# In-projection of a hybrid layer: 15 of its 20 units issued from a timetable, weight differences kept between the halves

## The chip, the core and the metric

The kernel runs on one core of a Trainium2 chip. The core has a matrix engine (TensorE, PE in the rows), three engines for elementwise work (VectorE or DVE, ScalarE or ACT, GpSimd or POOL) and a queue that issues DMA transfers (SyncE, SP). Each engine takes its instructions strictly in the order in which they were put into its queue, so an instruction that waits holds up everything behind it. The metric is the device time of one execution in microseconds, the median over runs.

## The reference, cut to what matters

The reference is one layer over 2048 time steps of 1024 channels: a normalised input, one wide projection, three recurrent mixers, an output projection and a gated convolutional feed-forward part. The change stands in the wide projection and in the causal convolutions that follow it.

```python
h = rms_norm(x, norm_mix_pre[l])                                     # x: (1, 2048, 1024) float32
xm, om, im, fm, xr, yr, zs, xbcs, dts = split_cols(h @ w_in[l])
# mLSTM:  x_c = silu(causal_dwconv(x_m, conv_w, conv_b))             # four taps each
# RG-LRU: xc  = causal_dwconv(x_r, conv_w, conv_b);  ... gelu(y_r)
# SSD:    xbc = silu(causal_dwconv(xbc, conv_w, conv_b))
def rms_norm(x, g):
    return x * lax.rsqrt(jnp.mean(x * x, axis=-1, keepdims=True) + EPS) * g
```

## The kernel before, in words

The products are float32. Each operand is cut into a high part and a low part (`hi` on ScalarE, L132, and `lo`, the rest, L134), and three matmuls with a moving block of 128x512 make one product (`split3`, L109 to L111).

Columns that are needed with time along the free axis are computed in two halves of 1024 time steps (half one, half two), each in ten **units**, b = 0 to 9. A unit gives two blocks of 128 output channels for 1024 steps. It is a Strassen product in Winograd's form: seven products of size 128 x 512 over four depth steps, so 7 x 4 x 3 = 84 matmuls. The seven run in the order b11, b21, T4, T1, T2, b22, T3, named by their weights; X, Y, V and Z are the PSUM banks that they add into. T1 to T4 are differences of weight blocks (`sub`, L139, on VectorE): T1 = b12 - b11, T2 = b22 - T1, T4 = T2 - b21, T3 = b22 - b12. They depend on the weights alone, and both halves compute them.

Four times in a unit ScalarE copies a bank out of PSUM (`keep`, L369): p1 after product one, p5 after product four, u2 after five and u3 after seven. Product six adds into bank Z only after p5 has been copied, product seven into bank X only after u2. Four adds on VectorE (L420 to L440) make the unit's two blocks ca and cb.

Around this run, in the same queues:
- the causal convolution of the unit before: per block a scale with bias on ScalarE (L448), three taps on VectorE (L451; in half two also three short ones on the carried tail, L455), for most blocks a Silu on ScalarE (L766, L771), and a store to `PT` (L778);
- the weights of a later unit: two loads of 512 KB (`ra`, `rb`, L270, L272), four differences, seven `hi`, seven `lo`, the latter on GpSimd;
- in half one, units 1 to 8, one tile of the input for half two (`norm_tile`, L613): a load, a square with its sum and a square root on ScalarE (L94, L95), a scaling on VectorE (L622), eight 128x128 transposes on TensorE (L628), two products with the gain on VectorE (L629) and a store of 512 KB;
- in half two, units 0 to 8, one step each of the gates' computation (`gates`, L644).

The order in each queue is the work of a list scheduler in the kernel's framework. It knows estimated durations and the priority of an instruction, which is its place in the program; PSUM evictions are given a higher one (`high_priority`). `t_units` (L736) calls the units in turn, and `between(b)` (L911 for half one, L951 for half two) puts the tile or the gate step behind unit b.

Of the kernel before, what the change touches and what calls it, by code (L numbers as in the profile page):

```python
# [9 lines left out]
F32 = mybir.dt.float32  # L10
F32R = mybir.dt.float32r
AF = mybir.ActivationFunctionType
# [51 lines left out]
def tile_hymba_layer(ctx: ExitStack, tc: tile.TileContext, io, out, scr):  # L64
    nc = tc.nc
    PSUM = bass.MemoryType.PSUM

    const = ctx.enter_context(tc.tile_pool(name="const", bufs=1))

    def c_tile(shape, name, dt=F32):  # L70
        return const.tile(shape, dt, name=name, tag=name)
# [16 lines left out]
    def col(t, name, j=0, n=1):  # L88
        o = COLS[name][0] + j
        return t[:, o : o + n]  # L90
# [493 lines left out]
    def phase_i():  # L584
# [141 lines left out]
        def gate_consts(gp):  # L726
# [6 lines left out]
            nc.vector.tensor_scalar_mul(nsp8, sp8, -8.0)  # L733
            nc.vector.tensor_scalar_mul(sp8, sp8, 8.0)

        def t_units(half, tp, tu, between=None, tail=None, w=None):  # L736

            t0 = half * TH
            w = w or prod.weights(tp, io["win_u"][0], f"iw{half}_0", half == 1, ON_DVE if half else ())
            if half == 1:  # L740
                for k in range(4):
                    prod.block(1, k, "a22", nc.vector if k % 2 else nc.gpsimd)
            for b in range(10):
                nm = f"i{half}_{b}"
                if b > 0:
                    w = prod.weights(tp, io["win_u"][b], f"iw{half}_{b}")
                pair = prod.unit(tu, w, nm, None, half == 1 and b == 0)
                if between is not None:
                    between(b)
                if tail is not None and b == 9:  # L750
                    tail()
                for i, c_ in enumerate(pair):
                    blk = 2 * b + i
                    if blk < 4:
                        nc.sync.dma_start(scr["PT"][4 + blk, :, t0 : t0 + TH], c_)
                    if blk < 16:
                        wn, bn, cb = (
                            ("cmw", "cmb", blk) if blk < 4 else ("crw", "crb", blk - 4) if blk < 8
                            else ("csw", "csb", blk - 8)
                        )  # L760
                        u = conv(
                            tu, c_, [col(par, wn, 4 * cb + k) for k in range(4)], col(par, bn, cb),
                            tails[:, blk, :], half, f"{nm}u{i}",
                        )
                    if blk < 4:
                        nc.scalar.activation(u, u, AF.Silu)  # L766
                        dst = blk
                    elif blk < 8:
                        dst = 16 + blk - 4
                    elif blk < 16:  # L770
                        nc.scalar.activation(u, u, AF.Silu)  # L771
                        dst = blk
# [88 lines left out]
        def in_proj_0():  # L861
# [46 lines left out]
            cnt = ExitStack()  # L908
            nt = open_pool(cnt, "nt", "right")

            def between(b):  # L911
                if 0 < b < 9:
                    norm_tile(nt, NCH + b - 1, load_x(nt, NCH + b - 1, 1), 2)()
                elif b == 9:
                    cnt.close()
                    pools.append(open_pool(ctu, "npa0", "right"))
                    st.append(n_units(pools, 0, range(NA, 4), [pu], "pu", 6, NRAW0))
                    next(st[0])
# [20 lines left out]
        def in_proj_1():  # L939
            ctp, ctu = ExitStack(), wo_ctx  # L940
            tu = open_pool(ctu, "bpp", "right")
            prep_pool.append(tu)
            prod.cps, prod.ws = CPS, 14 if W_EARLY else 18
            cgp = ExitStack()
            tp = open_pool(ctp, "tp1")
            gp = open_pool(cgp, "gp0")
            steps = gates(0, gp, pu, "px")

            st, pools = [], []

            def between(b):  # L951
# [457 lines left out]
    NJ = NFF // 2  # L1409
    NU = 8  # L1410

    dram = ctx.enter_context(tc.tile_pool(name="dram", bufs=1, space=bass.MemoryType.DRAM))
    aS = dram.tile([NU, P, NJ, 7, P], F32, name="aS", tag="aS")
    W = {}
    A = {}
# [981 lines left out]
```

## Time and profile before

| | |
|---|---|
| median of three runs | 2641.61 us (2638.68 to 2641.89) |
| time of the profiled execution | 2638.97 us |
| its span, first to last instruction | 2637.1 us |
| busy: TensorE, VectorE, ScalarE, GpSimd | 93%, 75%, 53%, 29% of the span |
| mean granted clock of TensorE | 0.977 of full speed |

Busy shares are means over the whole program, in which the in-projection's two halves fill 0.5 ms. What bounds this part is read from its own stretches: for each stretch the busy time of each engine and the granted clock (PEclk, 1.00 is 2.4 GHz), and TensorE's waits with the instruction that ended each.

### The profile page before, as it was taken

Reading aid. Unit: us, or ns where it says so; the run is one execution under the profiler, and the core shown is the slowest. Engines: PE = TensorE matmul, PEld = TensorE weight load, DVE = VectorE, ACT = ScalarE, POOL = GpSimd, SP = SyncE. Lnnn points to the kernel's source line nnn. Section 1 sums busy time; section 2 is a strip of 40 time slices with the busy share of each in tenths; the row PEclk is TensorE's granted clock in tenths of the full one; section 3 lists DMA queues with packets and bytes.
Section 4 is the critical chain, followed back from the end, with each engine's and each line's share of the span. In section 5 each row is a group of like instructions: output and inputs, shape, how many; then the busy total and the mean of one; then the engine's idle time right before and its main releaser. Section 6 shows DMA issues by size and latency. Waiting matters only on the chain. (4 is left out here: it accounts for less than half of the span.)

```text
span 2637.1 us, 38638 instructions
## 1 busy us (share of the span) xinstructions
PE 2459.5 (93%) x13658; PEld 2122.8 (80%) x13658; DVE 1986.0 (75%) x3096; ACT 1404.5 (53%) x2480; POOL 759.5 (29%) x616
## 2 busy tenths in 40 slices
PE   8899979899889989999899999989999988999997
PEld 8677867778788878877688787768888878999997
DVE  6898688857889864465787988877877877556676
ACT  5546655445467676555544544554445455445443
POOL 5555444434344442122500000111010143003222
PEclk9999989999999999999999999999999999999999
DMA  7444643236566555475645655656666658768875
GB/s 249 142 164 138 201 148 130 93 122 196 167 177 188 170 187 172 156 245 178 218 152 163 198 191 192 222 193 215 196 187 208 190 192 316 228 209 269 278 264 200
DMA packets 316338, 507.79 MB, mean 193 GB/s; under 512 B 23616, under 2 KB 198976, under 8 KB 316144
## 3 DMA queue, kind: packets, MB, share of 16 engines
q1 hardware_dynamic: 315152, 502.17, 58.9%
q8 instruction: 107, 1.75, 0.3%
q0 software_dynamic: 704, 2.10, 0.2%
q10 hardware_dynamic: 288, 1.05, 0.1%
q14 instruction: 87, 0.71, 0.1%
HBM read 337.72 MB, written 167.51 MB: 192 GB/s over the span
## 5 line engine op out<-in xcount | busy, mean ns | idle before, releaser
L997 POOL TENSOR_TENSOR yn<-yn,yg 128x512 f32<-128x512 f32 x16 | 22.1, 1380 | 149.4 <-DMA yg<-gate 93.2
L2209 POOL TENSOR_TENSOR o<-o,y 128x512 f32<-128x512 f32 x14 | 24.3, 1737 | 124.7 <-DVE y L2208 25.2
L109 PE MATMUL mix<-wo,ym 128*128 128x512 f32 x128 | 51.9, 405 | 1.6 <-DVE ysl L1028 1.6
L111 PE MATMUL mix<-wo,ym 128*128 128x512 f32 x128 | 50.9, 398 | 0.0
L110 PE MATMUL mix<-wo,ym 128*128 128x512 f32 x128 | 50.6, 395 | 0.0
L110 PE MATMUL mix<-wol,ysh 128*128 128x512 f32 x128 | 50.2, 392 | 0.1
L111 PE MATMUL mix<-woh,ysl 128*128 128x512 f32 x128 | 49.9, 390 | 0.0
L109 PE MATMUL mix<-woh,ysh 128*128 128x512 f32 x128 | 49.5, 392 | 0.2 <-ACT woh L580 0.2
L2103 POOL TENSOR_TENSOR d_0l<-d_0r,d_0h 128x768 fp32r<-128x768 f32 x2 | 4.1, 2074 | 145.7 <-DVE e_6y L2185 144.2
L1510 DVE TENSOR_TENSOR bh<-hT,g 128x512 f32<-128x512 f32 x32 | 20.7, 684 | 31.8 <-PE hT L1509 31.8
L999 DVE TENSOR_TENSOR yn<-yn,yg 128x1024 f32<-128x1024 f32 x16 | 21.3, 1330 | 22.0 <-ACT yg L998 22.0
L1028 DVE TENSOR_TENSOR ym<-yT,ym 128x512 fp32r<-128x512 f32 x16 | 11.0, 689 | 34.3 <-ACT ym L1027 34.3
L2118 ACT ACTIVATE e_8h<-e_8a 128x896 fp32r<-128x896 f32 x15 | 14.3, 954 | 36.9 <-DMA e_8a<-aS 28.8
L2119 DVE TENSOR_TENSOR e_10l<-e_10a,e_10h 128x896 fp32r<-128x896 f32 x15 | 16.4, 1090 | 23.3 <-ACT e_10h L2118 23.2
L1499 ACT ACTIVATE bt<-bx 128x1024 f32<-128x1024 f32 x16 | 16.9, 1059 | 29.4 <-DVE bx L1498 29.4
L852 ACT ACTIVATE no<-n 128x256 f32<-128x256 f32 x64 | 23.8, 374 | 16.2 <-PE n L111 5.9
L628 PE MATMUL xT<-ident,x 128*128 128x128 f32 x128 | 20.3, 305 | 12.8 <-DVE x L622 8.4
L629 DVE TENSOR_TENSOR hT<-xT,par 128x512 f32<-128x512 f32 x32 | 21.4, 683 | 13.6 <-PE xT L628 13.6
L998 ACT ACT_TABLE_LOAD x16 | 20.5, 1283 | 19.7 <-DMA yg<-gate 19.5
L2119 DVE TENSOR_TENSOR e_6l<-e_6a,e_6h 128x896 fp32r<-128x896 f32 x15 | 23.9, 1590 | 8.6 <-ACT e_6h L2118 8.6
L2119 DVE TENSOR_TENSOR e_5l<-e_5a,e_5h 128x896 fp32r<-128x896 f32 x15 | 23.2, 1547 | 8.6 <-ACT e_5h L2118 8.6
L2119 DVE TENSOR_TENSOR e_9l<-e_9a,e_9h 128x896 fp32r<-128x896 f32 x15 | 16.4, 1090 | 17.6 <-ACT e_9h L2118 17.6
(11864 smaller groups left out, 10855.1 us busy)
## 6 DMA issues: line engine op xcount, KB each, us to landing
x<-in_x_dram SPq DMA_DIRECT2D x16, 512.0 KB, 5.9
hT<-hT SPq DMA_DIRECT2D x16, 512.0 KB, 4.2
gate<-no SPq DMA_DIRECT2D x64, 128.0 KB, 2.9
yn<-yns SPq DMA_DIRECT2D x16, 512.0 KB, 4.7
yg<-gate SPq DMA_DIRECT2D x16, 512.0 KB, 5.1
bx<-in_x_dram SPq DMA_DIRECT2D x16, 512.0 KB, 5.1
x<-bx SPq DMA_DIRECT2D x16, 512.0 KB, 2.9
h2T<-bh SPq DMA_DIRECT2D x16, 512.0 KB, 5.0
```

The lines of the kernel that those rows point to most:

```text
L109: a = nc.tensor.matmul(pss, lh, rh, start=first, stop=False, skip_group_check=True)
L110: nc.tensor.matmul(pss, lh, rl, start=False, stop=False, skip_group_check=True)
L111: nc.tensor.matmul(pss, ll, rh, start=False, stop=last, skip_group_check=True)
L628: nc.tensor.transpose(pt[:, j * P : (j + 1) * P], xt[:, k * P : (k + 1) * P], ident)
L629: nc.vector.tensor_tensor(hT[:, 4 * q : 4 * q + 4], pt.rearrange("p (a b) -> p a b", a=4), col(par, "g1", 4 * q, 4).unsqueeze(2).to_broadc ...
L852: nc.scalar.activation(o, pt[:, 0:256], AF.Copy)
L997: nc.gpsimd.tensor_tensor(yn[:, 512:], yn[:, 512:], g[:, 512:], op=ALU.mult)
L998: nc.scalar.activation(g, g, AF.Sigmoid)
L999: nc.vector.tensor_tensor(yn, yn, g, op=ALU.mult)
L1510: nc.vector.tensor_tensor(hT[:, q * 4 : q * 4 + 4, :], pt.rearrange("p (a b) -> p a b", a=4), g2[:, 4 * q : 4 * q + 4].unsqueeze(2).to_bro ...
L2119: nc.vector.tensor_tensor(al, a, ah.bitcast(F32), op=ALU.subtract)
L2209: nc.gpsimd.tensor_tensor(o[i][:, hs], o[i][:, hs], t, op=ALU.add)
```

## The change

Units 1 to 8 of half one and 1 to 7 of half two no longer go through the scheduler. `timed_units` gives each instruction a time in slots: a slot is one depth step of a product (three matmuls), 28 slots make a unit, `t0` is a unit's start and `t1` its end. All instructions are sorted by these times and issued in that order, as it stands, to their engines' queues (`manual_schedule`). With that:
- all of a unit's evictions, convolutions and stores, the weights of the next unit (prepared 28 slots ahead), the input tiles and the gate steps stand at fixed slots;
- `lo` is computed on VectorE, except that of b11 in half one, which stays on GpSimd;
- the tile's eight transposes stand inside product six, and its gains are eight 128x128 copies with a column scale on ScalarE instead of two products on VectorE;
- in half one the differences T1 to T4 of the units prepared by the timetable (2 to 9) are also stored to DRAM (`iT`, 256 KB each); in half two those of units 2 to 8 are loaded instead of computed, and the fourth weight block b12 is not loaded.

Unit 0 and unit 9 of both halves and unit 8 of half two stay with the scheduler. The matmuls themselves and their order are unchanged.

```diff
--- before.py
+++ after.py
+        iT = dram.tile([10, P, 4, 512], F32, name="iT", tag="iT")
+        def timed_units(half, tp, tu, units, between, w):
...
+            def unit_events(b):
+                t0 = 28 * b
+                t1 = t0 + 28
...
+                for q, (bk, wn, hn, first) in enumerate((
+                    ("X", "b11", "a11", True), ("Y", "b21", "a12", True), ("V", "T4", "a22", True),
+                    ("Z", "T1", "s1", True), ("X", "T2", "s2", False), ("Z", "b22", "s4", False),
+                    ("X", "T3", "s3", False),
+                )):
+                    for k in range(4):
+                        at(t0 + 4 * q + k, step, bk, wn, hn, first, k)
...
+                at(t0 + 4, keep, "p1", "X")
+                at(t0 + 9.8, c_of, 0)
+                at(t0 + 9.9, evac, 0, 0, "Y", "p1")
+                at(t0 + 16, keep, "p5", "Z")
+                at(t0 + 20, keep, "u2", "X")
+                at(t0 + 24.1, c_of, 1)
+                at(t0 + 24.2, evac, 1, 0, "Z", "u2")
+                at(t1, keep, "u3", "X")
+                at(t1, evac, 1, 1, "X", "p5")
+                at(t1 + 0.9, evac, 0, 1, "u3", "V", ALU.subtract)
...
+                for i, (tc0, taps, tf) in enumerate(((2, (4.2, 6.1, 8.0), 10.2), (3.8, (12.4, 14.3, 16.2), 18.3))):
+                    blk = 2 * b + i
+                    if blk < 4:
+                        at(t1 + 2 + i, store, i, 4 + blk, "c")
...
+                    at(t1 + tc0, conv0, i, blk)
+                    for sh in (1, 2, 3):
+                        at(t1 + taps[sh - 1], tap, i, blk, sh)
+                    if blk < 4 or blk >= 8:
+                        at(t1 + tf, func, i, AF.Silu)
+                    at(t1 + tf + 1.6, store, i, blk if blk < 4 or blk >= 8 else 16 + blk - 4, "u")
...
+            def weight_events(b):
+                t0 = 28 * (b - 1)
...
+                at(t0 - 14, load, "ra", slice(0, 2), ("b11", "b21"))
+                at(t0 - 12, load, "rb", slice(2, 3 if half else 4), ("b22",) if half else ("b22", "b12"))
+                if half:
+                    for i, t in ((4, -11), (1, -8), (2, 3), (3, 10)):
+                        at(t0 + t, load_t, i)
+                    names = ("T4", "T1", "b11", "b21", "T2", "b22", "T3")
+                    his, los = (-1, 2.5, 5.5, 9, 13, 17, 20.5), (1.8, 3.6, 10.8, 11.6, 18.1, 20, 25.2)
+                else:
+                    at(t0 + 1.8, diff, "T1", "b12", "b11")
+                    at(t0 + 2.6, diff, "T2", "b22", "T1")
+                    at(t0 + 3.4, diff, "T4", "T2", "b21")
+                    at(t0 + 20.2, diff, "T3", "b22", "b12")
+                    at(t0 + 5.1, store_t, 1, 2, 4)
+                    at(t0 + 21.2, store_t, 3)
+                    names = ("b11", "b21", "T4", "T1", "T2", "b22", "T3")
+                    his, los = (-2, 3, 5, 9, 12.5, 17, 21.5), (-1, 10.8, 11.6, 18.1, 21.2, 22, 25.2)
+                for i, (name, th, tl) in enumerate(zip(names, his, los)):
+                    at(t0 + th, hi, name)
+                    at(t0 + tl, lo, name, nc.vector if i or half else nc.gpsimd)
+            for b in units:
+                unit_events(b)
+                between(b, at)
+            for b in units[1:]:
+                weight_events(b)
+            weight_events(units[-1] + 1)
+            with tc.manual_schedule():
+                for _, _, f, args in sorted(ev, key=lambda e: e[:2]):
+                    f(*args)
+            return W_[units[-1] + 1]
...
+            timed = range(1, 8 if half else 9)
             for b in range(10):
                 nm = f"i{half}_{b}"
-                if b > 0:
+                if b == 1:
+                    w = prod.weights(tp, io["win_u"][1], f"iw{half}_1")
+                    w = timed_units(half, tp, tu, timed, between, w)
+                if b in timed:
+                    continue
...
-                    norm_tile(nt, NCH + b - 1, load_x(nt, NCH + b - 1, 1), 2)()
...
+                    def scale():
+                        nc.vector.reciprocal(xn["ss"], xn["ss"])
+                        nc.vector.tensor_scalar_mul(xn["x"], xn["x"], xn["ss"])
+                    def transposes(q):
+                        xn[q] = pu.tile([P, 512], F32, name=f"xT{tt}_{q}", tag="px", bufs=2)
+                        for j in range(4):
+                            k = q * 4 + j
+                            nc.tensor.transpose(
+                                xn[q][:, j * P : (j + 1) * P], xn["x"][:, k * P : (k + 1) * P], ident
+                            )
+                    def gains(q):
+                        if q == 0:
+                            xn["h"] = nt.tile([P, KT, P], F32, name=f"hT{tt}", tag="hT", bufs=2)
...
+                            nc.scalar.activation(
+                                xn["h"][:, k], xn[q][:, j * P : (j + 1) * P], AF.Copy, scale=col(par, "g1", k)
+                            )
...
+                    at(t0 - 2, load)
+                    at(t0 + 7, square)
+                    at(t0 + 19, scale)
+                    at(t0 + 22.5, transposes, 0)
+                    at(t0 + 23.5, transposes, 1)
+                    at(t0 + 24.3, gains, 0)
+                    at(t0 + 25.8, gains, 1)
+                    at(t0 + 29, store)
...
+                if at is not None:
+                    at(28 * b + 22, next, steps, None)
+                    return
```

ScalarE in half one, while TensorE is in products four to seven of unit 6; iw0_7 are the weights of unit 7, i0_5 and i0_6 units 5 and 6. Before:

```order
L132 ACTIVATE iw0_7T2h_2220<-iw0_7T2_2208 128x512
L771 ACT_TABLE_LOAD
L771 ACTIVATE i0_5u0_1998<-i0_5u0_1998 128x1024
L369 ACTIVATE i0_6p5_2111<-i0_6Z_2058 128x512
L771 ACTIVATE i0_5u1_2006<-i0_5u1_2006 128x1024
L132 ACTIVATE iw0_7b22h_2224<-iw0_7rb_2196 128x512
L132 ACTIVATE iw0_7T3h_2230<-iw0_7T3_2228 128x512
L369 ACTIVATE i0_6u2_2125<-i0_6X_2056 128x512
```

Now:

```order
L871 ACTIVATE iw0_7T1h_2166<-iw0_7T1_2110 128x512
L820 ACT_TABLE_LOAD
L820 ACTIVATE i0_5u0_2112<-i0_5u0_2112 128x1024
L871 ACTIVATE iw0_7T2h_2186<-iw0_7T2_2117 128x512
L773 ACTIVATE i0_6p5_2204<-i0_6Z_2181 128x512
L871 ACTIVATE iw0_7b22h_2212<-iw0_7rb_2016 128x512
L820 ACTIVATE i0_5u1_2127<-i0_5u1_2127 128x1024
L773 ACTIVATE i0_6u2_2229<-i0_6X_2101 128x512
L871 ACTIVATE iw0_7T3h_2238<-iw0_7T3_2231 128x512
L1119 ACTIVATE hT13_2263<-xT13_0_2245,par_114 128x128 x4
```

The first Silu of unit 5 and the high part of T2 changed places, the second Silu went behind the high part of b22, and the first four of the eight gains (hT13) follow T3.

VectorE in half two, from behind the first add of unit 5 to the second (i1_5cb, now i1_5c1). Before:

```order
L451 SCALAR_TENSOR_TENSOR i1_4u1_4389<-i1_4cb_4270,par_112,i1_4u1_4389 128x1023
L455 SCALAR_TENSOR_TENSOR i1_4u1_4389<-tails_115,par_112,i1_4u1_4389 128x1
L451 SCALAR_TENSOR_TENSOR i1_4u1_4389<-i1_4cb_4270,par_112,i1_4u1_4389 128x1022
L455 SCALAR_TENSOR_TENSOR i1_4u1_4389<-tails_115,par_112,i1_4u1_4389 128x2
L451 SCALAR_TENSOR_TENSOR i1_4u1_4389<-i1_4cb_4270,par_112,i1_4u1_4389 128x1021
L455 SCALAR_TENSOR_TENSOR i1_4u1_4389<-tails_115,par_112,i1_4u1_4389 128x3
L139 TENSOR_TENSOR iw1_7T1_4743<-iw1_7rb_4733,iw1_7ra_4731 128x512
L139 TENSOR_TENSOR iw1_7T2_4745<-iw1_7rb_4733,iw1_7T1_4743 128x512
L139 TENSOR_TENSOR iw1_7T4_4747<-iw1_7T2_4745,iw1_7ra_4731 128x512
L139 TENSOR_TENSOR iw1_7T3_4765<-iw1_7rb_4733 128x512
L434 TENSOR_TENSOR i1_5cb_4440<-i1_5Z_4443,i1_5u2_4510 128x512
```

Now:

```order
L874 TENSOR_TENSOR iw1_6b11l_4554<-iw1_6ra_4436,iw1_6b11h_4553 128x512
L874 TENSOR_TENSOR iw1_6b21l_4574<-iw1_6ra_4436,iw1_6b21h_4573 128x512
L807 SCALAR_TENSOR_TENSOR i1_4u1_4540<-i1_4c1_4499,par_114,i1_4u1_4540 128x1023
L811 SCALAR_TENSOR_TENSOR i1_4u1_4540<-tails_117,par_114,i1_4u1_4540 128x1
L807 SCALAR_TENSOR_TENSOR i1_4u1_4540<-i1_4c1_4499,par_114,i1_4u1_4540 128x1022
L811 SCALAR_TENSOR_TENSOR i1_4u1_4540<-tails_117,par_114,i1_4u1_4540 128x2
L807 SCALAR_TENSOR_TENSOR i1_4u1_4540<-i1_4c1_4499,par_114,i1_4u1_4540 128x1021
L811 SCALAR_TENSOR_TENSOR i1_4u1_4540<-tails_117,par_114,i1_4u1_4540 128x3
L874 TENSOR_TENSOR iw1_6T2l_4600<-iw1_6T2_4537,iw1_6T2h_4599 128x512
L874 TENSOR_TENSOR iw1_6b22l_4625<-iw1_6rb_4448,iw1_6b22h_4624 128x512
L709 TENSOR_TENSOR lf0_4320<-bc0_4321,mst0_4486 4x1024
L779 TENSOR_TENSOR i1_5c1_4666<-i1_5Z_4590,i1_5u2_4641 128x512
```

The four differences of unit 7 (L139) are gone. Four low parts of unit 6's weights (L874) stand around unit 4's taps, and the first row of a gate step (L709) ahead of the second add.

SP's queue in half one, the transfers issued for one unit. Before:

```order
L270 DMA iw0_6ra_2014<-in_win_u_dram 128x1024
L272 DMA iw0_6rb_2016<-in_win_u_dram 128x1024
L609 DMA x11_1796<-in_x_dram 128x1024
L640 DMA hT_58<-hT10_1626 128x8x128
L778 DMA PT_59<-i0_3u0_1640 128x1024
L778 DMA PT_59<-i0_3u1_1647 128x1024
```

Now:

```order
L852 DMA iw0_6ra_1816<-in_win_u_dram 128x1024
L852 DMA iw0_6rb_1827<-in_win_u_dram 128x1024
L823 DMA PT_59<-i0_3u1_1749 128x1024
L865 DMA iT_120<-iw0_5T3_1851 128x512
L610 DMA x12_1899<-in_x_dram 128x1024
L1124 DMA hT_58<-hT11_1883 128x8x128
L865 DMA iT_120<-iw0_6T1_1920 128x512
L865 DMA iT_120<-iw0_6T2_1927 128x512
L865 DMA iT_120<-iw0_6T4_1935 128x512
L823 DMA PT_59<-i0_4u0_1922 128x1024
```

Four stores of differences (iT) joined the six transfers. The load of the input tile (x12) stands behind the store of T3 and a store of the unit-3 block.

## Rows read from the trace of the kernel before

**Rows 1.** Stretches of the in-projection; columns named in the fence's first line
```profile
core 0: us, PE busy (x) PEld busy (x) DVE busy (x) ACT busy (x) POOL busy (x), PEclk, DMA share, GB/s
102.64:277.06 174.42, 164.17 (x737) 131.88 (x736) 144.30 (x153) 99.74 (x146) 91.93 (x55) 1.00 0.46 151
256.81:277.06 20.25, 20.25 (x95) 16.53 (x94) 13.38 (x17) 13.51 (x19) 9.29 (x6) 1.00 0.55 168
391.52:575.66 184.14, 167.94 (x677) 133.39 (x678) 155.18 (x180) 90.45 (x129) 82.73 (x56) 0.93 0.28 102
391.52:397.20 5.68, 5.68 (x14) 4.48 (x15) 5.64 (x12) 0.54 (x1) 0.00 (x0) 0.51 0.19 76
440.36:459.80 19.44, 19.44 (x87) 15.90 (x86) 17.42 (x18) 9.19 (x13) 9.55 (x6) 1.00 0.34 107
459.80:479.09 19.29, 19.29 (x86) 15.77 (x84) 17.93 (x22) 9.12 (x14) 11.26 (x7) 1.00 0.23 85
```

**Rows 2.** TensorE's waits, half one, units 1 to 8; total, times, longest
```profile
PE i_1Z L109 <- ACT i_1p L369: 2.4, 1, 2.4
PE i_2Z L109 <- ACT i_2p L369: 1.8, 1, 1.8
...
PE i_5Z L109 <- ACT i_5p L369: 0.6, 1, 0.6
```

**Rows 3.** TensorE's waits before and in units 1 to 8, half two
```profile
PE i_1X L109 <- DVE i_0u L385: 6.9, 1, 6.9
PE i_5Z L109 <- ACT i_5p L369: 5.5, 1, 5.5
PE i_2Z L109 <- ACT i_2p L369: 2.8, 1, 2.8
...
PE i_7Z L109 <- ACT i_7p L369: 1.0, 1, 1.0
```

**Rows 4.** Order of time on ScalarE, half one, unit 6; start, duration
```profile
224.20 1.28 ACT L771 ACT_TABLE_LOAD   x1
...
226.46 0.58 ACT L369 ACTIVATE i_6p<-i_6Z 128x512 f32<-128x512 f32 x1
228.89 1.07 ACT L771 ACTIVATE i_5u<-i_5u 128x1024 f32<-128x1024 f32 x1 [1.85 <-DVE i_5u L451]
...
230.90 0.57 ACT L369 ACTIVATE i_6u<-i_6X 128x512 f32<-128x512 f32 x1
```

**Rows 5.** Order of time on VectorE, the same unit
```profile
221.33 1.27 DVE L451 SCALAR_TENSOR_TENSOR i_5u<-i_5cb,par,i_5u 128x1023 f32<-128x1023 f32 x1
222.53 2.31 DVE L451 SCALAR_TENSOR_TENSOR i_5u<-i_5ca,par,i_5u 128x1021 f32<-128x1021 f32 x1
...
228.86 0.67 DVE L139 TENSOR_TENSOR iw_8T<-iw_8rb,iw_8T 128x512 f32<-128x512 f32 x1
229.45 0.74 DVE L622 TENSOR_SCALAR x<-x,xss 128x1024 f32<-128x1024 f32 x1
```

**Rows 6.** Order of time on GpSimd, the same unit
```profile
222.13 1.62 POOL L134 TENSOR_TENSOR iw_7T1l<-iw_7T,iw_7T1h 128x512 fp32r<-128x512 f32 x1 [2.46 <-ACT iw_7T1h L132]
```

**Rows 7.** Order of time on ScalarE, half two, unit 6
```profile
523.39 1.06 ACT L771 ACTIVATE i_5u<-i_5u 128x1024 f32<-128x1024 f32 x1 [4.24 <-DVE i_5u L455]
...
524.87 0.58 ACT L369 ACTIVATE i_6u<-i_6X 128x512 f32<-128x512 f32 x1
```

**Rows 8.** A source line on VectorE; duration min/median/max
```profile
L166 DVE TENSOR_TENSOR iA_0a11a11l<-iA_2a,iA_0a11a11h x1: 680/680/680, 345.8 to 345.8; 128x512 fp32r<-128x512 f32 x1
```

**Rows 9.** A source line on ScalarE; duration min/median/max
```profile
L1222 ACT ACTIVATE m_0hs<-m_0pn,m_0dn x16: 346/367/375, 609.8 to 924.5; 128x128 f32<-128x128 f32 x16
```

**Rows 10.** VectorE's groups, half one, units 1 to 8; busy, mean, idle before
```profile
L629 DVE TENSOR_TENSOR hT<-xT,par 128x512 f32<-128x512 f32 x15 | 10.3, 685 | 12.4 <-PE xT L628 12.4
```

**Rows 11.** ScalarE's groups, the same stretch
```profile
L94 ACT ACTIVATE xj<-x 128x1024 f32<-128x1024 f32 x7 | 7.4, 1054 | 9.1 <-DMA x<-in_x_dram 9.1
```

**Rows 12.** DMA issues of the whole span; KB each, median us to landing
```profile
x<-in_x_dram SPq DMA_DIRECT2D x16, 512.0 KB, 5.9
```

More of the change, by code (lines that the diff above doesn't have):

```diff
@@ L68, in tile_hymba_layer @@
     const = ctx.enter_context(tc.tile_pool(name="const", bufs=1))
+    dram = ctx.enter_context(tc.tile_pool(name="dram", bufs=1, space=bass.MemoryType.DRAM))
     def c_tile(shape, name, dt=F32):
@@ L742, in t_units @@
                     prod.block(1, k, "a22", nc.vector if k % 2 else nc.gpsimd)
+            timed = range(1, 8 if half else 9)
             for b in range(10):
                 nm = f"i{half}_{b}"
-                if b > 0:
+                if b == 1:
+                    w = prod.weights(tp, io["win_u"][1], f"iw{half}_1")
+                    w = timed_units(half, tp, tu, timed, between, w)
+                if b in timed:
+                    continue
+                if b > timed[-1] + 1:
                     w = prod.weights(tp, io["win_u"][b], f"iw{half}_{b}")
@@ L909, in in_proj_0, with between, load, square @@
             nt = open_pool(cnt, "nt", "right")
-            def between(b):
+            def between(b, at=None):
                 if 0 < b < 9:
-                    norm_tile(nt, NCH + b - 1, load_x(nt, NCH + b - 1, 1), 2)()
+                    tt, xn = NCH + b - 1, {}
+                    t0 = 28 * b
+                    def load():
+                        xn["x"] = load_x(nt, tt, 1)
+                    def square():
+                        xn["ss"] = ip.tile([P, 1], F32, name=f"xss{tt}", tag="xss", bufs=4)
+                        jk = nt.tile([P, D], F32, name=f"xj{tt}", tag="xj", bufs=1)
+                        nc.scalar.activation(jk, xn["x"], AF.Square, accum_out=xn["ss"])
+                        nc.scalar.activation(xn["ss"], xn["ss"], AF.Sqrt, scale=1.0 / D, bias=epst)
+                    def scale():
[7 more added lines that the diff above has]
+                                xn[q][:, j * P : (j + 1) * P], xn["x"][:, k * P : (k + 1) * P], ident
+                            )
+                    def gains(q):
+                        if q == 0:
+                            xn["h"] = nt.tile([P, KT, P], F32, name=f"hT{tt}", tag="hT", bufs=2)
+                        for j in range(4):
+                            k = q * 4 + j
+                            nc.scalar.activation(
+                                xn["h"][:, k], xn[q][:, j * P : (j + 1) * P], AF.Copy, scale=col(par, "g1", k)
+                            )
+                    def store():
+                        nc.sync.dma_start(scr["hT"][:, :, tt * P : (tt + 1) * P].rearrange("k p t -> p k t"), xn["h"])
+                    at(t0 - 2, load)
[6 more added lines that the diff above has]
+                    at(t0 + 29, store)
                 elif b == 9:
@@ L949, in in_proj_1, with between @@
             st, pools = [], []
-            def between(b):
+            def between(b, at=None):
+                if at is not None:
+                    at(28 * b + 22, next, steps, None)
+                    return
                 next(steps, None)
@@ L1410, in tile_hymba_layer @@
     NU = 8
-    dram = ctx.enter_context(tc.tile_pool(name="dram", bufs=1, space=bass.MemoryType.DRAM))
     aS = dram.tile([NU, P, NJ, 7, P], F32, name="aS", tag="aS")
```

76 lines of the change are left out of this document (added).

## The prediction

> **What bounds the kernel now.** I read the stretches first, then TensorE's waits in them, then the order of time around a wait. The stretch of units 1 to 8 of half one lasts 174.42 us, with VectorE busy for 144.30 and ScalarE for 99.74; unit 8 alone, in which TensorE waits for nothing, takes 20.25 us with its tile's transposes in it [rows 1]. Half two's units 1 to 8 last 184.14 us, while two of them, without transposes, run in 19.44 and 19.29 us [rows 1]. So TensorE's own work is the floor of both halves, and the distance to it is 174.42 - 8 x 20.25 = 12.4 us in half one and 184.14 - 8 x 19.37 = 29.2 us in half two.
>
> What fills that distance: in half one seven waits, from 2.4 down to 0.6 us, 10.2 us together [rows 2]; the other 2.2 us are small gaps. In half two the seven waits inside units 1 to 8, from 5.5 to 1.0 us, make 16.3 us, and a further 6.9 us wait stands before unit 1 [rows 3]. The granted clock over half two's stretch is 0.93, in half one 1.00 [rows 1]: 0.07 x 184.14 = 12.9 us, which with 16.3 gives the 29.2. In the 5.68 us after the 6.9 us wait the clock is 0.51, near the lower of the two levels [rows 1]. Waits of up to 2.4 us in half one left the clock at 1.00; the lost clock belongs to half two's longer waits.
>
> Nearly all these waits are for a copy out of PSUM on ScalarE, and ScalarE is not busy then: it is blocked. In unit 6 of half one the copy i_6u starts at 230.90, behind a Silu that waited 1.85 us for a tap on VectorE [rows 4]. In half two the Silu at 523.39 waited 4.24 us and the copy i_6u came behind it [rows 7]. The taps are late because of their neighbours: a tap that takes 1.27 us takes 2.31 where a `lo` runs on GpSimd at the same time [rows 5, 6]. VectorE, stretched and in an unlucky order, sets the Silus; the Silus set ScalarE; ScalarE sets the banks.
>
> **The change part by part.** *lo from GpSimd to VectorE.* One `lo` on VectorE takes 0.68 us [rows 8]. Half one pays 6 x 0.68 = 4.1 us a unit for it, half two 7 x 0.68 = 4.8. What it gives back is the stretching, some 1.04 us for each tap that met one (2.31 - 1.27).
>
> *VectorE's sum per unit afterwards.* Half one: six taps at 1.27 = 7.6, four adds and four differences of the same shape at 0.67 = 5.4, six `lo` = 4.1, the scaling 0.74 [rows 5, 8], together 17.9 of 20.25 us; before it was busy 144.30 / 8 = 18.0 [rows 1], with the gains in it, two of 0.685 us [rows 10], which go. Half two: taps 7.6, adds 2.7, `lo` 4.8 = 15.1 us, and the tails and a gate step beside them in the remaining 4.3; before 155.18 / 8 = 19.4, all of its unit. The differences that are no longer computed take 4 x 0.67 = 2.7 us a unit off. So VectorE fits under TensorE in both halves, with more room in half two.
>
> *Gains on ScalarE.* The nearest row for a 128x128 copy with a column scale out of PSUM is 0.37 us [rows 9]; eight are 2.9 us. Unit 8's 13.51 us [rows 1] become 16.4 of 20.25. From both sides: a quarter of the 0.685 us that VectorE takes for 128x512 [rows 10] would make 1.4 us in all, 0.685 us each 5.5 and thus 19.0, still under the unit. I take 2.9. ScalarE's table loads stay as many as they were, at 1.28 us [rows 4]. The Trainium skill, "ScalarE: Activation LUTs", section "Rules for kernel authors", budgets about 2.7 us for each switch to another table set. Here a load is followed by its Silu within 1.29 us of its start [rows 4], so the trace disagrees; by the page two switches a unit would add 2.8 us and bring ScalarE to 19.2, with hardly any slack, which is the first rival's case.
>
> *The order.* By the slots a copy is due four slots (4 x 19.37 / 28 = 2.8 us) before TensorE needs its bank: p5 at 16, needed at 20; u2 at 20, needed at 24. Adding up durations in the order of each queue, I find p5 done about two slots and u2 about one and a half before they are needed in half one, earlier in half two. The tightest place is the tile: the scaling ends some 0.5 us before the transposes at slot 22.5. If the scaling is late, TensorE waits by as much in each of eight units.
>
> *DRAM instead of differences.* Half one adds four stores of 256 KB a unit, half two takes four loads and drops a quarter of `rb`. Half one moved 151 GB/s at a DMA share of 0.46 [rows 1], 3.3 MB a unit; with 1.0 MB more the share becomes about 0.6. The trace has no transfer of 256 KB like these. The nearest is 512 KB in 5.9 us to landing [rows 12]; from below, half of that. The loads stand ten slots (6.9 us) ahead of their first reader, so even at 5.9 us they are hidden: cost nothing. Without that cover it would be some 3 us a unit.
>
> *What stays.* The 6.9 us wait before unit 1 of half two hangs on unit 0's chain on VectorE, which the scheduler still orders, and the slow clock behind it: 5.68 x 0.49 = 2.8 us. Units 0 and 9 I leave as they are; unit 8 of half two is cheaper as its weights and unit 7's work no longer stretch VectorE.
>
> **Sum.** Half one -12.4. Half two -29.2 + 2.8 = -26.4. Against that I set 0.2 us a unit, some 3.2 us in all, for small slips, half the 0.5 us of the tile's margin. Together -35.6. From the profiled execution's 2638.97 us this is 2603.4; the median of the runs lies 2.6 us above the profiled execution, so 2606. The case's own range is 2596 to 2614.
>
> **Rivals.** *One: the timetable frees only half two.* In half one ScalarE takes 2.9 us more, and every Silu and the square still stand ahead of copies. If one slips, the fixed order can't give way: half one stays at 174.4. For it: VectorE at 17.9 of 20.25 leaves little room. Against it: both are under the floor. Time: -26.4 + 1.6 = -24.8, so 2617. Half one alone gained, with half two unchanged, is -12.4 + 1.6, so 2631: the loads from DRAM would have to come late.
>
> *Two: slower, by the tile's load.* The tile has one buffer. Its load can go out only when the transposes of the tile before are done, about 2.5 us before the unit's end, and it stands on SP behind the store of T3. With 5.9 us [rows 12] it lands 3.4 us into the unit. The square waits for it on ScalarE, and behind it stand T1's high part, the table load, a Silu, T2's and then p5, some 6.8 us of work, with p5 needed 13.6 us into the unit. So it decides from about 3.4 us of further lateness on; beyond that TensorE waits for each us in each of eight units. For it: before, the square already waited 9.1 us in seven units for this tile [rows 11], and the queue gets four more transfers a unit. Against it: a share of 0.6 leaves the DMA engines room. To end above the old time it must cost over 36 / 8 = 4.5 us a unit, a landing after 13.8 us or so; at 16 us it is 8 x 6.7 = 54 us on the 2606, or 2660.
>
> *Three: no gain.* What the in-projection gives back is lost behind it, because the recurrences wait for something else: 2642. Against it: TensorE is busy for 93% of the span and the next part takes its input from these units.
>
> **Chances.** The forecast 0.62, half two alone 0.20, half one alone 0.05, the slow tile 0.08, nothing 0.05. Faster by more than 0.2%, which is 5.3 us and about what a measurement of this kernel can tell from no change: 0.62 + 0.20 + 0.05 = 0.87; within it 0.05; slower 0.08. The range runs from 2592, if the 6.9 us wait and its slow clock shrink too and nothing slips (2638.97 - 38.8 - 9.7 + 2.6 = 2593), to 2631 with half two unchanged; the slow tile and part of no gain are left out.
>
> **What would show it.** Right: half one's units 1 to 8 near 162 to 164 us and half two's near 158 to 160, taps at 1.27 us throughout, no wait of TensorE for p5 or u2, and a granted clock of 1.00 behind the first 6 us of half two. A wait of the transposes for the scaling in each unit would put the allowance too low. Waits for ScalarE's copies in half one with ScalarE busy would speak for the first rival, a square that waits long for its tile for the second. I am wrong if the in-projection gets as short as this and the total doesn't follow.

## The result: 2641.75 to 2607.27 us

Over four runs each the kernel before has a median of 2641.75 us (2638.68 to 2645.34) and the changed one 2607.27 us (2605.82 to 2608.33), a ratio of 0.9863 with a 95% interval of 0.9843 to 0.9883. Measured again later, it had 2606.29 against 2643.68 us, 0.9851 (0.9821 to 0.9881). The forecast was 2606 us, its range 2592 to 2631. One execution of all those below, 7472 us for the kernel before with an unused DRAM tile, was a slow one and stands in no figure.

The stretches of units 1 to 8 in the changed kernel's profile, as in [rows 1], and the first 6 us of half two's stretch:

```profile
core 0: us, PE busy (x) PEld busy (x) DVE busy (x) ACT busy (x) POOL busy (x), PEclk, DMA share, GB/s
98.33:260.15 161.82, 161.82 (x738) 132.40 (x736) 137.20 (x191) 119.95 (x214) 10.35 (x8) 1.00 0.62 211
374.38:531.88 157.50, 157.12 (x677) 127.59 (x678) 130.13 (x203) 90.04 (x127) 4.73 (x4) 0.99 0.46 149
374.38:380.40 6.02, 6.02 (x20) 4.87 (x21) 5.14 (x8) 2.04 (x2) 0.00 (x0) 0.75 0.33 129
```

Half one's eight units take 161.82 us instead of 174.42, which is 8 x 20.23 with no wait of TensorE at all. Half two's take 157.50 instead of 184.14. ScalarE is busy for 119.95 / 8 = 15.0 us a unit in half one, VectorE for 137.20 / 8 = 17.2; GpSimd fell from 91.93 us to 10.35. TensorE's waits before and in half two's units, as in [rows 3]:

```profile
PE i_1X L110 <- DVE i_0u L386: 4.1, 1, 4.1
PE ptr L683 <- DVE r L685: 0.4, 1, 0.4
```

The wait of unit 1 is still there, 4.1 us instead of 6.9, and the clock behind it is 0.75 for 6.0 us instead of 0.51 for 5.7. ScalarE in unit 6 of half one, as in [rows 4], start and duration first:

```profile
205.47 1.05 ACT L1099 ACTIVATE xj<-x 128x1024 f32<-128x1024 f32 x1
...
208.75 1.28 ACT L820 ACT_TABLE_LOAD   x1
210.04 1.06 ACT L820 ACTIVATE i_5u<-i_5u 128x1024 f32<-128x1024 f32 x1
...
211.53 0.58 ACT L773 ACTIVATE i_6p<-i_6Z 128x512 f32<-128x512 f32 x1
...
213.50 1.06 ACT L820 ACTIVATE i_5u<-i_5u 128x1024 f32<-128x1024 f32 x1 [0.87 <-DVE i_5u L807]
214.47 0.58 ACT L773 ACTIVATE i_6u<-i_6X 128x512 f32<-128x512 f32 x1
...
216.10 2.17 ACT L1119 ACTIVATE hT<-xT,par 128x128 f32<-128x128 f32 x8
```

The first Silu starts without a wait at 210.04, and the copy i_6p follows at 211.53. The second Silu still waits 0.87 us for a tap, and the copy i_6u comes at 214.47; TensorE waits for neither copy. The eight gains take 2.17 us. VectorE in the same unit, as in [rows 5]:

```profile
203.69 3.92 DVE L807 SCALAR_TENSOR_TENSOR i_5u<-i_5c,par,i_5u 128x1023 f32<-128x1023 f32 x3
...
208.95 0.68 DVE L874 TENSOR_TENSOR iw_7T4l<-iw_7T,iw_7T4h 128x512 fp32r<-128x512 f32 x1
209.55 3.92 DVE L807 SCALAR_TENSOR_TENSOR i_5u<-i_5c,par,i_5u 128x1023 f32<-128x1023 f32 x3
...
214.18 0.75 DVE L1104 TENSOR_SCALAR x<-x,xss 128x1024 f32<-128x1024 f32 x1
```

Three taps in a row take 3.92 us, 1.31 each, with no 2.31 among them, and a `lo` takes 0.68. Of the 84 taps of units 1 to 7 in both halves 83 take 1.27 to 1.29 us and one 2.39. The scaling ends at 214.93 us; the transposes that need it start at 215.35, so the margin is 0.42 us.

Where the time came from, stage by stage, from the two profiled executions (the end of a stage is the next one's first matmul):

| stage | before | changed | difference |
|---|---|---|---|
| half one, unit 0 | 32.30 | 28.10 | -4.2 |
| half one, units 1 to 8 | 174.42 | 161.82 | -12.6 |
| half two, unit 0 and the wait behind it | 33.44 | 32.95 | -0.5 |
| half two, units 1 to 8 | 184.14 | 157.50 | -26.6 |
| end of half two's unit 9 | 595.12 | 551.34 | -43.8 |
| from there to the end of the span | 2041.98 | 2052.76 | +10.8 |

The stages that are not listed changed by 0.3 us or less. By the end of the in-projection 43.8 us are gained, 33.0 by the end of the span. Of the part behind, this is before's stretch in one row of the windows:

```profile
595.12:2637.10 2041.98, 1928.57 (x11046) 1678.75 (x11044) 1523.70 (x2538) 1086.60 (x1975) 469.66 (x409) 0.98 0.63 204
```

So 10.8 us seem to be given back where no engine's order differs. The experiments below ask whether that is so.

### The profile page after: what moved, and what is told of

Its sections match the earlier page's. It is cut to its first block, busy times and chain, and to the rows that moved or that the text cites. A ratio compares the mean times of both kernels' runs of the same rounds, so it can differ in the third digit from the quotient of the medians.

```text
span 2604.1 us, 38618 instructions
## 1 busy us (share of the span) xinstructions
PE 2451.1 (94%) x13658; PEld 2121.9 (81%) x13658; DVE 1953.2 (75%) x3149; ACT 1425.2 (55%) x2546; POOL 604.4 (23%) x519
## 5 line engine op out<-in xcount | busy, mean ns | idle before, releaser
L2431 POOL TENSOR_TENSOR o<-o,y 128x512 f32<-128x512 f32 x14 | 24.6, 1759 | 126.5 <-DVE y L2430 26.6
L1029 ACT ACTIVATE no<-n 128x256 f32<-128x256 f32 x64 | 23.9, 375 | 16.4 <-PE n L112 7.2
L110 PEld LDWEIGHTS mix<-wo,ym 128*128 128x128 f32 x128 | 24.5, 192 | 6.9 <-issue 1.7
L110 PEld LDWEIGHTS mix<-woh,ysh 128*128 128x128 f32 x128 | 24.2, 190 | 6.8 <-ACT woh L581 1.5
L2341 DVE TENSOR_TENSOR e_9l<-e_9a,e_9h 128x896 fp32r<-128x896 f32 x15 | 16.4, 1091 | 17.7 <-ACT e_9h L2340 17.6
```

Source lines behind the costliest of these rows:

```text
L110: a = nc.tensor.matmul(pss, lh, rh, start=first, stop=False, skip_group_check=True)
L1029: nc.scalar.activation(o, pt[:, 0:256], AF.Copy)
L2341: nc.vector.tensor_tensor(al, a, ah.bitcast(F32), op=ALU.subtract)
L2431: nc.gpsimd.tensor_tensor(o[i][:, hs], o[i][:, hs], t, op=ALU.add)
```

## The experiments

Theory one, the prediction's: a `lo` on GpSimd stretches VectorE's taps beside it, and moving it is what frees TensorE. Theory two: the fixed order frees it, and the placement only gives slack. "Half one" and "half two" below are units 1 to 8 of each.

**The changed kernel again**, unchanged, with a new profile.

> The changed kernel once more. In its first profile units 1 to 8 of half one took 161.8 us, those of half two 157.5, and from the end of the in-projection's last unit to the end of the span 2052.8 us, against 2042.0 before, though every engine's order there is the same. If the 10.8 us belong to the change, this profile has 2050 to 2055 there again; if they belong to that one execution, it lies near 2042 to 2047 and the total near 2600.

Measured: half one 161.81 us, half two 158.78, behind the in-projection 2053.9 us; the median of its four runs was 2606.29. The stages repeat, half two within 1.3 us.

**The kernel before again**, one run.

> The kernel before once more, for a second profile. Units 1 to 8 at 174.4 and 184.1 us and 2042 us behind the in-projection if these stages repeat; a spread of several us behind it would make the 10.8 us a matter of the execution.

Measured: 174.64 and 180.63 us, 2038.8 behind, 2632.6 us in all. Half two differs by 3.5 us from the first profile of the same kernel. Behind the in-projection before has 2042.0 and 2038.8 now, the changed kernel 2052.8 and 2053.9.

**The timetable alone**, with all placements of before.

```diff
-at(t0 + tl, lo, name, nc.vector if i or half else nc.gpsimd)
+at(t0 + tl, lo, name, nc.gpsimd)
-# gains(q): four nc.scalar.activation(hT[k], xT[k], AF.Copy, scale=g1[k])
+# gains(q): one nc.vector.tensor_tensor(hT[4q:4q+4], xT, g1[4q:4q+4], op=mult)
-at(t0 + t, load_t, i)                     # half two; and store_t in half one
+at(t0 - 3, diff, "T1", "b12", "b11"); ...  # differences computed in both halves
...                                        # b12 loaded in half two too, its first hi half a slot later
```

> The timetable alone: lo back on GpSimd, gains back on VectorE, the differences computed in both halves. Theory one (lo on GpSimd stretches the taps; moving it is what frees TensorE): taps at 1.3 to 2.4 us again, half one 170 to 174 us, half two 178 to 184, total 2630 to 2642. Theory two (the fixed order frees TensorE, the placement only gives slack): half one 162 to 165, half two 158 to 162, total 2605 to 2615.

Measured over four runs: 2668.22 us, a ratio of 1.0091 (1.0061 to 1.0122): slower than before. The two stretches:

```profile
99.60:289.33 189.73, 172.93 (x737) 139.38 (x736) 150.84 (x159) 103.11 (x150) 87.94 (x56) 0.95 0.42 142
403.65:594.74 191.09, 170.13 (x678) 134.48 (x678) 160.50 (x182) 90.46 (x129) 84.75 (x55) 0.93 0.28 98
```

VectorE around one tile's scaling in unit 5:

```profile
198.25 5.73 DVE L807 SCALAR_TENSOR_TENSOR i_4u<-i_4c,par,i_4u 128x1023 f32<-128x1023 f32 x3
...
204.72 5.73 DVE L807 SCALAR_TENSOR_TENSOR i_4u<-i_4c,par,i_4u 128x1023 f32<-128x1023 f32 x3
...
210.56 0.75 DVE L1104 TENSOR_SCALAR x<-x,xss 128x1024 f32<-128x1024 f32 x1
```

Three taps take 5.73 us instead of 3.92, the scaling comes at 210.56, 17.8 us into a unit that started at 192.78, and the transposes inside product six wait for it:

```profile
PE xT L1110 <- DVE x L1104: 14.6, 7, 2.6
```

Seven waits of some 2 us, and behind them a clock of 0.95 over the stretch. Both theories had both halves and the total too low. What it shows goes further than theory one said: this timetable does not only fail to help without the placement, it costs 15.3 us in half one, since it puts the transposes where a late VectorE stops TensorE, and 7.0 us in half two.

**The placement alone**, under the scheduler of before, for the units whose weights the timetable prepares.

```diff
-w = prod.weights(tp, io["win_u"][b], f"iw{half}_{b}")
+w = prod.weights(tp, io["win_u"][b], f"iw{half}_{b}", False, on_dve,  # the seven names; in half one without b11
+                 diffs=iT[b] if half else None, save=None if half else iT[b])
-nc.vector.tensor_tensor(hT[4q:4q+4], pt, g1, op=mult)
+for j in range(4): nc.scalar.activation(hT[k], pt[k], AF.Copy, scale=g1[k])
```

> The placement alone, under the scheduler of before: lo on VectorE, gains on ScalarE, differences stored in half one and loaded in half two. Theory one: taps at 1.27 us, half one 162 to 166 us, half two 158 to 164, total 2605 to 2615. Theory two: the scheduler still puts Silus ahead of copies, half one 170 to 176, half two 172 to 184, total 2620 to 2645.

Measured: 2617.89 us median, 0.9895 (0.9864 to 0.9925), 2607.38 in the profiled execution.

```profile
100.14:263.43 163.29, 161.61 (x738) 132.78 (x736) 138.99 (x189) 115.60 (x205) 9.29 (x8) 1.00 0.63 214
344.83:383.65 38.82, 22.93 (x88) 17.89 (x87) 33.15 (x53) 20.74 (x37) 22.43 (x17) 0.78 0.43 142
383.65:538.92 155.27, 155.22 (x677) 126.23 (x675) 125.69 (x189) 88.68 (x126) 4.56 (x4) 1.00 0.46 158
```

163.29 and 155.27 us: the scheduler comes within 1.5 us of both floors without any timetable, and all but one of its 96 taps take less than 1.3 us. Theory one's range holds for half one; half two came out below its range and the median 2.9 us above it. Theory two had both halves too slow. At the end of half two's unit 9 this kernel is 36.7 us ahead of before, the changed one 43.8. What it loses is mostly in unit 0 of half two, 38.82 us: a gate step's matmul stands in TensorE's queue ahead of unit 1 and waits for the chain on VectorE.

```profile
PE pcs L681 <- DVE ci L677: 10.8, 1, 10.8
```

**lo alone back on GpSimd**, in the timetable; one run, as the next two.

```diff
-at(t0 + tl, lo, name, nc.vector if i or half else nc.gpsimd)
+at(t0 + tl, lo, name, nc.gpsimd)
```

> The changed kernel with every lo back on GpSimd, all else as it is. If the lo on GpSimd is what costs: taps near 1.8 us mean again, half one 172 to 190 us, half two 165 to 185. If the gains and the differences from DRAM freed the units: half one and half two within 3 us of 161.8 and 157.5.

```profile
98.37:288.01 189.64, 173.13 (x737) 139.22 (x736) 141.04 (x143) 119.58 (x214) 86.88 (x56) 0.95 0.55 184
404.12:586.14 182.02, 165.28 (x677) 130.83 (x678) 138.19 (x154) 89.51 (x127) 80.59 (x54) 0.96 0.40 129
```

TensorE's longest waits in half one, seven of them:

```profile
PE xT L1110 <- DVE x L1104: 14.3, 7, 2.5
```

The time was 2659.70 us, in the next two runs 2618.55 and 2614.05, and 2641.85 for the kernel before beside them. The 48 taps of half one take 1.80 us on average, against 1.28 in the changed kernel. The whole loss of the timetable alone in half one (189.64 against 189.73) and 24.5 us in half two come from this one line. TensorE waits for no `lo`: in half one it waits for the tile's scaling, which stands behind the late taps, in half two mostly for copies on ScalarE, as before. What `lo` alone would bring under the scheduler was not tried; the placement alone moved all three parts at once.

**Differences computed in half two**, nothing stored in half one.

```diff
-for i, t in ((4, -11), (1, -8), (2, 3), (3, 10)):
-    at(t0 + t, load_t, i)
+at(t0 - 3, diff, "T1", "b12", "b11")
+at(t0 - 2.2, diff, "T2", "b22", "T1")
+at(t0 - 1.4, diff, "T4", "T2", "b21")
+at(t0 + 18.8, diff, "T3", "b22", "b12")
...                                        # b12 loaded again, the first hi half a slot later, no store_t
```

> The changed kernel, differences computed in half two as well, nothing stored in half one. VectorE's busy time in half two goes from 130.1 / 8 = 16.3 us a unit to 19.0 of 19.3. If that room matters, half two takes 160 to 170 us; if only the place of lo matters, 157 to 160. Half one 161.8 in either case, unless the stores had cost something there.

```profile
98.50:260.31 161.81, 161.81 (x737) 132.41 (x736) 137.23 (x191) 119.95 (x214) 10.39 (x8) 1.00 0.48 162
374.69:544.07 169.38, 159.58 (x678) 127.80 (x679) 147.16 (x231) 88.74 (x126) 3.38 (x3) 0.99 0.31 110
```

Half two 169.38 us, 11.9 more, with VectorE busy for 147.16 / 8 = 18.4 us a unit; its longest wait inside a unit is again the copy p5 of unit 5:

```profile
PE i_5Z L110 <- ACT i_5p L773: 3.5, 1, 3.5
```

The four stores a unit in half one cost nothing: 161.81 without them too, at a DMA share of 0.48 instead of 0.62. So the differences on VectorE do cost something in half two. Their sum is not what decides, since 18.4 us lie under the 19.29 of a unit: whether it is the room that is left or their place in VectorE's queue, this run doesn't tell.

**Gains back on VectorE.**

```diff
-nc.scalar.activation(xn["h"][:, k], xn[q][:, j * P : (j + 1) * P], AF.Copy, scale=col(par, "g1", k))   # x4
+nc.vector.tensor_tensor(xn["h"][:, 4 * q : 4 * q + 4], xn[q], g1[4 * q : 4 * q + 4], op=ALU.mult)
```

> The changed kernel with the gains back on VectorE, two products of 0.685 us for eight copies on ScalarE. VectorE at 18.5 of 20.2 us in half one: 162 to 164 us if there is room, 166 to 172 if the scaling or the adds come late. Half two unchanged at 157 to 159.

```profile
99.39:261.20 161.81, 161.81 (x737) 132.40 (x736) 149.34 (x205) 103.91 (x150) 9.09 (x7) 1.00 0.62 209
375.56:533.89 158.33, 157.78 (x677) 127.79 (x678) 130.19 (x203) 89.45 (x127) 4.62 (x4) 0.99 0.46 148
```

161.81 us with VectorE at 149.34 / 8 = 18.7 of 20.2 us: this part of the change is worth nothing here.

**The tile's load later**, to find how near the second rival was.

```diff
-at(t0 - 2, load)
+at(t0 + 5.5, load)
```

> The changed kernel with the input tile's load 7.5 slots later, behind the stores of T1, T2 and T4 in SP's queue, so issued some 3.5 us into the unit instead of 2.5 us before its end, and landed 8 to 9 us into it. By the prediction's working the square has to start by 6.8 us or the copy p5 comes late: TensorE should wait 1 to 2 us in each of eight units, half one 170 to 178. If ScalarE has more room than that, 161.8 to 165.

One run. The time was 2621.32 us. TensorE waits in three units of the eight, not in each:

```profile
PE i_2Z L110 <- ACT i_2p L773: 3.0, 1, 3.0
PE i_7Z L110 <- ACT i_7p L773: 1.8, 1, 1.8
PE i_6Z L110 <- ACT i_6p L773: 1.7, 1, 1.7
```

ScalarE in unit 6, which starts at 206.29:

```profile
215.33 1.06 ACT L1099 ACTIVATE xj<-x 128x1024 f32<-128x1024 f32 x1 [2.94 <-DMA x<-in_x_dram]
...
221.40 0.58 ACT L773 ACTIVATE i_6p<-i_6Z 128x512 f32<-128x512 f32 x1
```

The load was issued at 210.91, 4.6 us into the unit; the square starts 9.0 us into it, after a wait of 2.94, the copy p5 at 15.1, and TensorE waits 1.7 us. That puts p5's due time near 14 us and the path from the square's start to p5's end at 6.7 us, where the prediction had 13.6 and 6.8. The wait in unit 2, 3.0 us, also cost clock, 0.93 over that unit: it took 25.06 us, 4.8 more. The scheduler put some matmuls of unit 9 among those of unit 8 here, so the stretch to compare runs from unit 1 to the end of unit 9: 190.5 us instead of 181.3. The 9.2 us more are what the first expectation asked for, but they come from three units and the clock, not from a wait in each of the eight. The mechanism is real. In the changed kernel the load is issued 2.6 us before the unit's end (217.12, the unit ends at 219.69) and takes 4.1 us, so it lands some 1.5 us into the next; the square must start by 14 - 6.7 = 7.3 us. That is more than 5 us of room, where the prediction gave 3.4.

**The 10.8 us behind the in-projection: addresses?** The change adds a DRAM tile ahead of the others. The kernel before with that tile declared and never used:

```diff
+iT = dram.tile([10, P, 4, 512], F32, name="iT", tag="iT")
```

> The kernel before with the DRAM tile for the differences declared ahead of the others, but never used: only addresses in DRAM may move. From the first matmul of the mLSTM part to the first of the RG-LRU part that follows it, two profiles of before took 113.1 and 114.0 us, the changed kernels and variants 117.1 to 119.5. If the addresses cause it, 117 to 120 here; if something left over from the in-projection does, 113 to 114.

> The kernel before with the unused DRAM tile, timed. In its one look it took 2656 us and 2058 behind the in-projection, against 2642 and 2039 to 2042. If the addresses cost it: 2650 to 2657 again, a ratio of 1.003 to 1.006. If that was one execution's luck: 2640 to 2645.

The first run gave 2656.19 us, and behind the in-projection:

```profile
596.16:2654.30 2058.14, 1936.09 (x11046) 1686.20 (x11044) 1526.76 (x2538) 1086.72 (x1975) 469.31 (x409) 0.98 0.63 202
```

From the first matmul of the mLSTM part to the first of the RG-LRU part it took 117.0 us, as expected if the addresses cause it. Timed over eleven runs the same kernel has a median of 2648.29 against 2646.56 us, a ratio of 0.9999 (0.9981 to 1.0016): no difference, though its second profile again had 2058.1 behind and 117.7 for that part. The other side, the changed kernel with the differences kept inside a tile that before has too:

```diff
-iT = dram.tile([10, P, 4, 512], F32, name="iT", tag="iT")
+def iT(b, i):     # aS, the feed-forward part's tile, idle here, same place as before
+    return aS[b // 4].rearrange("p j s t -> p (j s t)")[:, b % 4 * 2048 + i * 512 : b % 4 * 2048 + i * 512 + 512]
```

> The changed kernel, the differences kept in the feed-forward part's DRAM tile aS, which is idle at that time, instead of in a tile of their own: every instruction in the same order, the DRAM tiles where the kernel before has them. If the addresses cost what stands behind the in-projection: 2039 to 2045 us there instead of 2053, the total 2592 to 2598, a ratio near 0.982. If they don't: 2606, 0.986.

Measured 2608.52 us, 0.9857 (0.9831 to 0.9883), and 2061.3 us behind, 116.6 for the part just named: nothing came back. With the addresses moved the total is the same, and with them moved back it is too: the address theory, mine, falls. What the runs do show is that the part behind takes 2039 to 2061 us in fourteen profiles whose engines have the same order there, and that beside these last kernels the kernel before alone ran from 2637.7 to 2652.9 us. In those 17 runs its median is 2646.56; less some 594 us to the end of the in-projection and the 1.9 us outside the span, that leaves 2051 us behind it. The two profiles of before, at 2042.0 and 2038.8, are then at the fast end of that spread, and most of the 10.8 us is likely a comparison with lucky executions. That is worked out from totals; no profile of a slower execution of the kernel before was taken. What sets the spread was not settled.

**lo of half two's unit 1 on VectorE too**, on top of that.

```diff
-w = prod.weights(tp, io["win_u"][1], f"iw{half}_1")
+w = prod.weights(tp, io["win_u"][1], f"iw{half}_1", False, ("b11", ..., "T3") if half else ())
```

> As the one above, and the seven lo of unit 1 in half two on VectorE as well: they run on GpSimd beside the chain of 128x96 instructions that TensorE waits 4 us for, seven of which take 0.70 us each there and one behind them 0.26. If the same stretching is at work, the chain gets some 7 us shorter for 4.8 us of lo, the wait before unit 1 falls to 1 to 2 us and the total by 2 to 4 us. If the chain is bound by itself, it gets 5 us later and the wait grows to 8 to 9 us.

In the changed kernel the chain's seven 128x96 instructions take 4.91 us; their durations are given as minimum, median and maximum in ns, and below them stands the last `lo` on GpSimd:

```profile
367.98 4.91 DVE L553 SCALAR_TENSOR_TENSOR sp0p<-sp0p,sp0z 128x96 f32<-128x96 f32 x7
L553 DVE SCALAR_TENSOR_TENSOR sp0p<-sp0p,sp0z x7: 257/259/1247, 368.0 to 372.6; 128x96 f32<-128x96 f32 x7
370.32 1.28 POOL L135 TENSOR_TENSOR iw_1T3l<-iw_1T,iw_1T3h 128x512 fp32r<-128x512 f32 x1
```

So the 0.70 us of the expectation is a mean of two kinds. The first three, beside a `lo` each, take 1.21 to 1.25 us, and each of them ends some 0.11 us after a `lo` ends; the other four come after the last `lo` has ended at 371.6 and take 0.26 each, like the eighth.

Here they take 0.24 to 0.26 each, the scheduler puts the `lo` between them and the add that TensorE waits for (i_0u) ahead of the chain's rest:

```profile
368.71 0.24 DVE L554 SCALAR_TENSOR_TENSOR sp0p<-sp0p,sp0z 128x96 f32<-128x96 f32 x1
368.88 0.68 DVE L136 TENSOR_TENSOR iw_1b22l<-iw_1rb,iw_1b22h 128x512 fp32r<-128x512 f32 x1
369.49 0.68 DVE L387 TENSOR_TENSOR i_0u<-i_0X,i_0p 128x512 f32<-128x512 f32 x1
```

```profile
341.58:370.22 28.64, 22.35 (x87) 17.07 (x85) 23.34 (x37) 20.60 (x37) 14.08 (x10) 0.88 0.41 132
370.22:528.37 158.15, 156.20 (x677) 126.40 (x678) 132.03 (x213) 91.53 (x130) 4.95 (x4) 1.00 0.46 156
```

TensorE no longer waits before unit 1. Unit 0 takes 28.64 us instead of 32.95 with its wait, and units 1 to 8 take 158.15 instead of 157.71, so 3.9 us are gained in the two. How much of that is the add's earlier place, this run doesn't separate from the stretching. The median is 2602.72 us, a ratio of 0.9832 (0.981 to 0.9855), 5.8 us below the same kernel without it and the lowest of all; the intervals overlap, the 3.9 us are read from one profile of each.

## Why the prediction was right, and where it was not

**The floors.** -12.4 us in half one and -26.4 in half two were forecast from the undisturbed units; -12.6 and -26.6 came. The copies p5 and u2 are in time as the summed queues said, ScalarE's 15.0 us a unit lies under the 16.4 forecast, in part because the eight gains take 2.17 us instead of 2.9, and VectorE's 17.2 lies under 17.9. One reading was wrong on the way: of half one's distance to its floor, 2.2 us were called small gaps. TensorE's busy time there is 164.17 us [rows 1], 2.2 above 8 x 20.25, so it is longer busy time.

**The cause.** Late taps beside `lo` on GpSimd: shown by the runs, one line of placement is worth 27.8 us in half one and 24.5 in half two under the timetable. In half one of that run the late taps reached TensorE through the tile's scaling, and not through Silu and copy as the prediction had it for the kernel before; that path shows in half two of the same run, and in the placement alone, though there with all three parts moved. The Trainium skill, "SBUF — State Buffer", section "Who interferes with whom", says that a VectorE instruction with two SBUF inputs contends with a GpSimd instruction that reads SBUF; the trace agrees, 1.27 to 2.31 us for a tap [rows 5, 6], 0.26 to some 1.2 for a 128x96 one. The prediction did not say how much each part brings: the gains' move brought nothing, the differences from DRAM 11.9 us in half two beside a `lo` that is already moved. And its phrase of "an unlucky order" gave the order a share that it does not have: the scheduler does as well in the eight units once the placement is given. What the timetable adds to the placement is mostly in unit 0 of half two, 32.95 against 38.82 us, where the placement alone is slower than before's 33.44.

**The allowance** of 3.2 us for slips was not needed: all eight units of half one take 20.22 to 20.24 us. The margin at the scaling, put at 0.5 us, measured 0.42.

**Unit 0 of half one** was left as it was, and gave 4.2 us: a term that was missed. Before, the first tile's square and root stood ahead of that unit's copy p5 on ScalarE:

```profile
91.52 1.04 ACT L94 ACTIVATE xj<-x 128x1024 f32<-128x1024 f32 x1
...
93.08 0.28 ACT L95 ACTIVATE xss<-xss,epst 128x1 f32<-128x1 f32 x1
...
93.79 0.57 ACT L369 ACTIVATE i_0p<-i_0Z 128x512 f32<-128x512 f32 x1
```

Now the tile belongs to unit 1's slots, and the copy comes earlier:

```profile
92.09 0.57 ACT L370 ACTIVATE i_0p<-i_0Z 128x512 f32<-128x512 f32 x1
```

TensorE's wait for it, before and now:

```profile
PE i_0Z L109 <- ACT i_0p L369: 3.2, 1, 3.2
PE i_0Z L110 <- ACT i_0p L370: 1.4, 1, 1.4
```

The clock over the unit is 0.88 instead of 0.84. That is read from the two traces, not tried by itself, and the tile's place is not all of it. The placement alone keeps the square and the root ahead of that copy, and its unit 0 takes 29.79 us, with a wait of 2.1 and a clock of 0.89. So some 1.7 us of the 4.2 go with the tile's place. The other 2.5 came without it: behind the wait product six took 5.3 us before and 2.9 in the placement alone, and why the clock was higher there stays open.

**The wait before unit 1 of half two** stays, as said; 4.1 us instead of 6.9, but unit 0 itself took 28.9 us instead of 26.5, so the two together are -0.5 us.

**The sum.** -35.6 us were forecast; the medians give -34.5 and -37.4. It comes out for a reason that is partly luck: 4.2 us of unit 0 and 3.2 of allowance were missed on one side, and on the other the step from the in-projection's end to the total, -41 us on average over two profiles each against some -36 in the medians. The third rival was a small part of the truth at most; how much of these 5 us is really given back behind the in-projection stays open, since one kernel's executions differ by more there.

**The rivals.** Half one did not stay: ScalarE has 5 us of room, and a Silu follows its table load within 1.29 us here too. The tile's load is more than 5 us from the point from which it decides. The second rival's price did not follow from its own terms: with 6.8 us of work and p5 needed at 13.6, a landing at 11.3 us, not 13.8, costs 4.5 us a unit, and one at 16 us costs 9.2, not 6.7, so 74 us and not 54. The trace of before has other transfers of 256 KB that could have bounded the new ones: the loads of `yr` have a median of 2.7 us to landing, those of `m_1x` 6.5. Nothing turned on it, since TensorE waits for none of the new ones.

## What to carry to other kernels

When an engine's instructions are stretched by a neighbour, look first at which engine the neighbour could run on: under the order by hand, one line of placement was worth more than the whole change, and the order by hand without the placement was worse than the scheduler's. Work out the floor of a stage from a unit that nothing disturbs, then check that each engine's sum for a unit lies under it after the change. That check is needed and not enough: with `lo` on GpSimd VectorE's sum was 141.04 / 8 = 17.6 of 20.2 us and half one still lost 27.8 us, because the scaling stood behind late taps. And compare a stage behind the change over several executions before explaining a difference there.

## What the runs showed of the hardware

- Instructions of next to no work are stretched most beside GpSimd: 128x96 ones on VectorE took 1.21 to 1.25 us beside a `lo` of 1.28, and ended some 0.11 us after it, against 0.26 with GpSimd free. The mean of a row hid it: 4.91 us for seven.
- Eight 128x128 copies with a column scale out of PSUM took 2.17 us on ScalarE, 0.27 each in a row, against 0.37 for one [rows 9].
- The same instruction order behind the in-projection took from 2039 to 2061 us.
